# A Strassen weight gradient: loads in program order, twenty-one pairs instead of twenty, and a new plan of visits

## The chip, the cores and the metric

One core of a Trainium2 chip. The metric is the time of one execution on the device in microseconds, the median of several runs; all runs told here are in the fast state. A profiled execution gives the trace; its span is about 1.8 us shorter than the time (166.3 against 168.07 us before, 164.9 against 166.66 after), because the time also holds what lies before the first and after the last instruction. In the views PE is TensorE (matmuls; PEld its weight loads), DVE VectorE, ACT ScalarE, POOL GpSimd, which issues most loads here, and SP SyncE, which issues the outputs. The program keeps its operands and sums in tiles of one memory, SBUF, and lets PE accumulate in tiles of another, PSUM; it calls those banks. A landing is the moment at which a load's data is complete.

## The reference

```python
def setup_inputs():
    batch, m, k, n = 16, 512, 1024, 768          # fp32 normal
def reference(input, grad_output):
    return np.einsum('bmk,bmn->kn', input, grad_output).astype(np.float32)
```

So OUT (1024 x 768) = X^T G with 8192 rows. The rows are cut into 64 slices of 128. The output has four quadrants, A and B above, C and D below, each 512 x 384, which is four PSUM banks of 128 x 384 a quadrant.

## The kernel before

X and G are read as fp32 and land as bf16 (the transfer casts: of the 58.72 MB that the page counts as read from HBM, the loads issued by GpSimd take 57.28 and land as 28.64); only G of slice 0 and X of slices 0 and 1 land as fp32 and are rounded by DVE and ACT. A *plain* slice costs 16 matmuls of 384 columns, four a quadrant. A *Strassen pair* of slices costs seven products of four matmuls, 28 instead of 32, but needs six sums on DVE first. `LOADS` says which pairs of slices are plain ("s") and which are Strassen pairs ("P").

The loads and the six sums of a pair:

```python
LOADS = "ssssssssPPPPPPPPPPPPPPPPPPPPssss"
...
ctx.enter_context(tc.manual_schedule(engines={E.PE, E.DVE, E.Activation}))
...
for u, kind in enumerate(LOADS):
    ...                                   # tiles xp, gp; 14 pairs are held
    if u >= MERGED:                       # one transfer for both slices of a pair
        nc.gpsimd.dma_start(out=gp, in_=G[rows, :]...)
        nc.gpsimd.dma_start(out=xp, in_=X[rows, :]...)
    for h in range(2): ...                # otherwise one transfer a slice, first G, then X

def sum_g1(i): tensor_add(ge[:, 0:2, :], ...)    # 768 wide
def sum_g2(i): tensor_add(ge[:, 2, :], ...)      # 384
def sum_g3(i): tensor_sub(g[:, 1:3, :], ...)     # 768, in place
def sum_x1(i): tensor_add(xe[:, 0:2, :], ...)    # 1024: the "wide X sum"
def sum_x2(i): tensor_add(xe[:, 2, :], ...)      # 512
def sum_x3(i): tensor_sub(x[:, 1:3, :], ...)     # 1024, in place
```

The program has two sets of four banks only (`bank0` to `bank7`). So a quadrant or a product (m, n, o, p, q) is *visited*: it takes a set, accumulates some slices, and closes: each bank is evicted, by DVE (add into the sum in SBUF) or by ACT (copy out, after the old sum had been copied in at the opening). `ORDER` is the plan of visits. A step `3A17!3,0,0,1` reads: do 3 waiting DVE jobs first; matmuls for A up to its 17th item; close, and put 3, 0, 0 and 1 further DVE jobs ahead of the evictions of its four banks. `A21:2!...` opens A with two banks for ACT. The DVE jobs come from one list: six sums a pair, then the shares that add the products into the quadrants.

```python
def shut(q):
    fill(ahead[q])                        # DVE jobs queued ahead of this eviction
    bank, _, act = banks[q]
    dst = sum_of(p, q)
    if act:         nc.scalar.copy(out=dst, in_=bank)
    elif fresh[p]:  nc.vector.tensor_copy(out=dst, in_=bank)
    else:           nc.vector.tensor_add(out=dst, in0=bank, in1=dst)
    if final and p in "ABCD":             # last visit: the bank's part of the output leaves
        nc.sync.dma_start(out=OUT[...], in_=dst)
```

The program fixes the order of PE, DVE and ACT (`manual_schedule`), and in the trace DVE keeps to its order also where it must wait: before the change it is idle for 0.79 us ahead of an eviction at 103.24 us, though the X which the next two sums read (L149, L154) had landed before 101.77, when the wide X sum of the same pair starts. The order of the loads was left to the scheduler: at the start it puts G of slice 3 ahead of X of slice 2, then it follows the program up to pair 23, and then it takes, for example, X of pairs 24 and 25 ahead of their G.

Of the kernel before, what the change touches and what calls it, by code (L numbers as in the profile page):

```python
# [7 lines left out]

P = 128

LOADS = "ssssssssPPPPPPPPPPPPPPPPPPPPssss"



ORDER = (
    "A1:4 C1:4!0,0,0,0 B2:4!0,0,0,0 A2 D1:2 A3!0,0,0,0 D2 D3 D4 C4:4!0,0,0,0 D5 B5:2 D6!0,0,0,0 "
    "B6 A6:2 B7 B8 A7 A8 A9!0,0,0,0 B9 C9:2 C10!0,0,0,0 B11 D11:2 B12 D13!0,0,0,0 A14:2 A15 B14 "
    "B16!0,0,0,1 C16:2!2,0,1,2 A16 A17 D17:4!3,0,1,2 A18!0,0,0,0 n2:4!0,0,1,0 o1:2 m2:4 o2 "
    "2o3!3,0,0,0 m3!0,0,0,0 q3:4!1,2,0,0 p1:4 p2 p4 3D20:3!3,0,0,1 p5 q5:2!2,0,0,0 A21:2!1,0,0,2 "
    "p6 o6:2!2,0,0,1 n6:2 3p7!2,1,0,0 n7 m7:2!2,1,0,1 n8 q8:2!2,0,0,1 D24:2!2,0,1,1 n9 "  # L20
    "o9:2!2,0,0,1 A25:2 2n10!2,0,0,0 A26 m10:2!2,0,0,1 p11:2 3A27!3,0,0,0 p12 D27:2!1,0,0,2 "
    "q12:2!1,0,1,1 p13 o13:3!3,0,2,1 p14 n13:2!1,0,0,1 m14:2!1,0,1,2 p15 D30:2!2,0,0,1 "
    "A31:2!1,1,0,2 q16:2!1,1,0,1 p16 n16:2!2,1,0,0 p17 1m17:2!2,0,0,1 o17:2!2,0,0,2 D34:2!1,0,1,1 "
    "p18 p19 A34:4!4,1,1,0 p20!0,0,0,0 D35:0 o20:2!2,0,0,1 q20:2!1,0,0,1 n20:2!0,1,0,1 "
    "D37!0,0,0,0 m20:4!0,0,1,0 A35:0 A36 B19:0 B20 A39 A41 A44!11,0,0,0 B23 C17:0 B24!2,0,0,0 "
    "C24!2,0,0,0 D44:0!4,0,0,0 "
).split()


SHARES = (  # L30
    "l20 l21 t20 t21 t22 t23 t30 t31 t32 t33 t10 t11 t12 t13 l22 l23 l10 l11 l12 l13 l30 l31 l32 "
    "l33 "
).split()

WARMUP = [512] * 10 + [128] * 2
PAIRS_HELD = 14
SUMS_HELD = 9

MERGED = 8


@with_exitstack
def kernel(
# [30 lines left out]
    SLOT = {"n": 0, "p": 1, "m": 2, "o": 3, "q": 4}  # L74

    E = mybir.EngineType
    ctx.enter_context(tc.manual_schedule(engines={E.PE, E.DVE, E.Activation}))

    xf = [pairs.tile([P, K], f32, name=f"xf{s}", tag="xp") for s in range(2)]
    gf = pairs.tile([P, N], f32, name="gf", tag="gp")  # L80
# [18 lines left out]
    xg = []  # L99
    for u, kind in enumerate(LOADS):  # L100
        pool = pairs if u else head
        xp = pool.tile([P, 2, K], bf16, name="xp", tag="xp")
        gp = pool.tile([P, 2, N], bf16, name="gp", tag="gp")
        if u >= MERGED:
            rows = slice(2 * u * P, 2 * (u + 1) * P)
            nc.gpsimd.dma_start(out=gp, in_=G[rows, :].rearrange("(p m) n -> p m n", m=2))  # L106
            nc.gpsimd.dma_start(out=xp, in_=X[rows, :].rearrange("(p m) k -> p m k", m=2))  # L107
        for h in range(2):
            s = 2 * u + h
            if s > 0 and u < MERGED:  # L110
                nc.gpsimd.dma_start(out=gp[:, h, :], in_=G[s * P : (s + 1) * P, :])  # L111
            if s > 1 and u < MERGED:
                nc.gpsimd.dma_start(out=xp[:, h, :], in_=X[s * P : (s + 1) * P, :])  # L113
# [275 lines left out]
```

## Time and profile before

| | before |
|---|---|
| time, median (range) | 168.19 us (168.03 to 168.38) |
| span of the profiled run | 166.3 us |
| matmuls, with 12 for warm-up | 963 |
| PE busy, DVE busy | 159.8, 118.6 us |
| last load lands | 142.9 us |
| first matmul after warm-up starts, last starts | 5.18, 162.84 us |

The prediction below shows the lines that carry the argument. One more, part 4 of the page, the chain of waits that ended last:

```profile
PE 76%; DVE 16%; DMA 5%; POOL 1%; issue 1%; DVEq 0%; POOLq 0%
```

The chain goes through PE for three quarters and leaves it for DVE for a sixth of the span. Those are the places where a matmul waited for a sum or for an eviction.

### The profile page before, as it was taken

To read this page: it belongs to the slowest core of one execution; us is meant where nothing else is said; L and a number is where in the kernel's file an instruction comes from. 1 tells how busy PE (TensorE), PEld (TensorE's weight loads), DVE (VectorE), ACT (ScalarE), POOL (GpSimd) and SP (SyncE) were. 2 spreads that over 40 slices of the span, in tenths; PEclk is the share of its full clock that TensorE was granted. 3 is DMA by queue.
4 is the path that set the end of the run, shared out by engine and by line. 5 is a ranking of instruction groups with operands and counts; after the bars stand their busy time and mean duration, and the time that the engine had idled before them with its cause. 6 is when DMAs were issued, how large, how long until landed. Compare 5 with 4: busy or idle time off the path is not lost.

```text
span 166.3 us, 2688 instructions
## 1 busy us (share of the span) xinstructions
PE 159.8 (96%) x963; PEld 93.5 (56%) x963; DVE 118.6 (71%) x240; ACT 87.6 (53%) x206; POOL 41.1 (25%) x81
## 2 busy tenths in 40 slices
PE   8799999999999999999999999899999999999992
PEld 2356656565655655665565655455656656565661
DVE  0400221121979879878979998989999899999992
ACT  3779413330486768755648476756677878100000
POOL 7444444544122222222212222222221000000000
PEclk9999999999999999999999999999999999999999
DMA  5999999999999999999999999999999999105555
GB/s 181 287 209 208 211 206 208 208 209 217 211 216 211 215 212 214 210 215 210 215 211 214 211 213 212 217 211 212 212 217 213 214 210 209 25 0 189 189 189 189
DMA packets 14124, 33.39 MB, mean 201 GB/s; under 512 B 1568, under 2 KB 5920, under 8 KB 14112
## 3 DMA queue, kind: packets, MB, share of 16 engines
q0 software_dynamic: 11088, 28.64, 88.5%
q1 hardware_dynamic: 2736, 3.54, 6.0%
q10 hardware_dynamic: 288, 1.05, 1.7%
q8 instruction: 7, 0.11, 0.3%
q14 instruction: 5, 0.04, 0.1%
HBM read 58.72 MB, written 3.15 MB: 372 GB/s over the span
## 4 chain that ended last, share of the span: by engine, by line
PE 76%; DVE 16%; DMA 5%; POOL 1%; issue 1%; DVEq 0%; POOLq 0%
PE bank L278 75%; DVE macc L296 5%; DMA xp<-in_input_dram 5%; DVE gp L140 2%; DVE xe L145 2%; DVE acc L296 2%; DVE ge L131 2%; DVE xp L154 1%; POOL gp L111 1%; DVE ge L135 1%; DVE xe L149 1%; PE bank L328 0%; DVE acc L336 0%; DVEq L296 0%; POOLq L373 0%
## 5 line engine op out<-in xcount | busy, mean ns | idle before, releaser
L278 PEld LDWEIGHTS <-xp 128*128 128x128 bf16 x697 | 67.6, 98 | 49.4 <-issue 1.9
L278 PE MATMUL bank<-gp,xp 128*128 128x384 bf16 x537 | 92.4, 326 | 2.0 <-DVE xp L203 0.8
L292 ACT COPY acc<-bank 128x384 f32<-128x384 f32 x55 | 24.4, 487 | 31.2 <-PE bank L278 31.1
L296 DVE TENSOR_TENSOR acc<-bank,acc 128x384 f32<-128x384 f32 x46 | 23.7, 552 | 21.3 <-PE bank L278 21.0
L292 ACT COPY macc<-bank 128x384 f32<-128x384 f32 x61 | 27.3, 492 | 20.2 <-PE bank L278 20.1
L278 PEld LDWEIGHTS <-xe 128*128 128x128 bf16 x240 | 23.2, 98 | 16.6 <-DVE xe L145 1.4
L278 PE MATMUL bank<-ge,xp 128*128 128x384 bf16 x160 | 29.8, 326 | 0.2
L278 PE MATMUL bank<-gp,xe 128*128 128x384 bf16 x160 | 28.3, 326 | 0.3 <-DVE xe L145 0.2
L296 DVE TENSOR_TENSOR macc<-bank,macc 128x384 f32<-128x384 f32 x37 | 19.4, 553 | 5.3 <-PE bank L278 5.0
L107 POOL DMA_DIRECT2D xp<-in_input_dram x24 | 12.7, 530 | 36.9 <-DMA xp<-in_input_dram 20.3
L106 POOL DMA_DIRECT2D gp<-in_grad_output_dram x24 | 12.7, 530 | 32.7 <-PE bank L278 19.5
L268 ACT COPY bank<-macc 128x384 f32<-128x384 f32 x43 | 19.3, 490 | 0.0
L268 ACT COPY bank<-acc 128x384 f32<-128x384 f32 x41 | 18.4, 501 | 0.0
L163 DVE TENSOR_TENSOR acc<-acc,macc 128x768 f32<-128x768 f32 x16 | 14.5, 950 | 0.0
L145 DVE TENSOR_TENSOR xe<-xp 128x1024 bf16<-128x1024 bf16 x20 | 13.7, 684 | 0.7 <-DMA xp<-in_input_dram 0.7
L278 PE MATMUL bank<-ge,xe 128*128 128x384 bf16 x80 | 14.1, 326 | 0.0
L154 DVE TENSOR_TENSOR xp<-xp 128x1024 bf16<-128x1024 bf16 x20 | 13.7, 683 | 0.0
L131 DVE TENSOR_TENSOR ge<-gp 128x768 bf16<-128x768 bf16 x20 | 11.0, 550 | 0.1
L140 DVE TENSOR_TENSOR gp<-gp 128x768 bf16<-128x768 bf16 x20 | 11.0, 551 | 0.0
L113 POOL DMA_DIRECT2D xp<-in_input_dram x14 | 7.5, 538 | 9.0 <-DMA xp<-in_input_dram 6.4
L111 POOL DMA_DIRECT2D gp<-in_grad_output_dram x15 | 8.2, 547 | 6.1 <-DMA gp<-in_grad_output_dram 4.6
L294 DVE COPY acc<-bank 128x384 f32<-128x384 f32 x2 | 1.0, 554 | 10.6 <-PE bank L278 10.6
(19 smaller groups left out, 34.3 us busy)
## 6 DMA issues: line engine op xcount, KB each, us to landing
xp<-in_input_dram POOLq DMA_DIRECT2D x24, 512.0 KB, 16.9
gp<-in_grad_output_dram POOLq DMA_DIRECT2D x24, 384.0 KB, 16.7
xp<-in_input_dram POOLq DMA_DIRECT2D x14, 256.0 KB, 8.5
gp<-in_grad_output_dram POOLq DMA_DIRECT2D x15, 192.0 KB, 8.5
out_dram<-acc SPq DMA_DIRECT2D x15, 192.0 KB, 1.9
xf<-in_input_dram ACTq DMA_DIRECT2D x2, 512.0 KB, 5.0
gf<-in_grad_output_dram SPq DMA_DIRECT2D x2, 192.0 KB, 4.3
out_dram<-acc SPq DMA_DIRECT2D x1, 128.0 KB, 1.7
```

Of the source, the lines that this page charges most:

```text
L106: nc.gpsimd.dma_start(out=gp, in_=G[rows, :].rearrange("(p m) n -> p m n", m=2))
L107: nc.gpsimd.dma_start(out=xp, in_=X[rows, :].rearrange("(p m) k -> p m k", m=2))
L111: nc.gpsimd.dma_start(out=gp[:, h, :], in_=G[s * P : (s + 1) * P, :])
L131: nc.vector.tensor_add(out=ge[:, 0:2, :], in0=g[:, :, 0, :], in1=g[:, :, 1, :])
L140: nc.vector.tensor_sub(out=g[:, 1:3, :], in0=g[:, 1:3, :], in1=g[:, 3::-3, :])
L145: nc.vector.tensor_add(out=xe[:, 0:2, :].rearrange("p a k -> p (a k)"), in0=xp[:, 0, :], in1=xp[:, 1, :])
L154: nc.vector.tensor_sub(out=x[:, 1:3, :], in0=x[:, 1:3, :], in1=x[:, 0::3, :])
L163: nc.vector.tensor_add(out=dst, in0=dst, in1=macc[:, slots, q, :])
L268: nc.scalar.copy(out=bank, in_=sum_of(p, q))
L278: nc.tensor.matmul(bank, stat, mov, start=opening and j == 0 and not carried, stop=close and j == len(items_now) - 1, skip_group_check=car ...
L292: nc.scalar.copy(out=dst, in_=bank)
L296: nc.vector.tensor_add(out=dst, in0=bank, in1=dst)
```

## The change

Its intent: let the transfers start in the order in which the program names them (GpSimd joins the engines whose order is fixed), turn one plain pair into a twenty-first Strassen pair (four matmuls fewer), merge the transfers of slices 14 and 15 too, and plan the visits anew on the landings measured on the chip. The whole diff:

```diff
--- before.py
+++ after.py
@@ -8,35 +8,34 @@
 
 P = 128
 
-LOADS = "ssssssssPPPPPPPPPPPPPPPPPPPPssss"
+LOADS = "ssssssssPPPPPPPPPPPPPPPPPPPPPsss"
 
 
 
 ORDER = (
-    "A1:4 C1:4!0,0,0,0 B2:4!0,0,0,0 A2 D1:2 A3!0,0,0,0 D2 D3 D4 C4:4!0,0,0,0 D5 B5:2 D6!0,0,0,0 "
-    "B6 A6:2 B7 B8 A7 A8 A9!0,0,0,0 B9 C9:2 C10!0,0,0,0 B11 D11:2 B12 D13!0,0,0,0 A14:2 A15 B14 "
-    "B16!0,0,0,1 C16:2!2,0,1,2 A16 A17 D17:4!3,0,1,2 A18!0,0,0,0 n2:4!0,0,1,0 o1:2 m2:4 o2 "
-    "2o3!3,0,0,0 m3!0,0,0,0 q3:4!1,2,0,0 p1:4 p2 p4 3D20:3!3,0,0,1 p5 q5:2!2,0,0,0 A21:2!1,0,0,2 "
-    "p6 o6:2!2,0,0,1 n6:2 3p7!2,1,0,0 n7 m7:2!2,1,0,1 n8 q8:2!2,0,0,1 D24:2!2,0,1,1 n9 "
-    "o9:2!2,0,0,1 A25:2 2n10!2,0,0,0 A26 m10:2!2,0,0,1 p11:2 3A27!3,0,0,0 p12 D27:2!1,0,0,2 "
-    "q12:2!1,0,1,1 p13 o13:3!3,0,2,1 p14 n13:2!1,0,0,1 m14:2!1,0,1,2 p15 D30:2!2,0,0,1 "
-    "A31:2!1,1,0,2 q16:2!1,1,0,1 p16 n16:2!2,1,0,0 p17 1m17:2!2,0,0,1 o17:2!2,0,0,2 D34:2!1,0,1,1 "
-    "p18 p19 A34:4!4,1,1,0 p20!0,0,0,0 D35:0 o20:2!2,0,0,1 q20:2!1,0,0,1 n20:2!0,1,0,1 "
-    "D37!0,0,0,0 m20:4!0,0,1,0 A35:0 A36 B19:0 B20 A39 A41 A44!11,0,0,0 B23 C17:0 B24!2,0,0,0 "
-    "C24!2,0,0,0 D44:0!4,0,0,0 "
+    "A1:4 C1:2!0,0,0,0 D1:2 A2!0,0,0,0 D2 B3:4 D3 D4!0,0,0,0 B4 C4:2 C5 B5 C6!0,0,0,0 B6 A6:2 B7 "
+    "A8!0,0,0,0 D8:2 B8 B9 D10!0,0,0,0 B10 B11 C7:2 C9 B12 C11 B13!0,0,0,0 C12 C13 A14:2 C14 "
+    "C16!0,0,0,0 A15 B16:2!3,0,0,0 D16:2 3A17!3,0,0,1 n2:4!0,1,1,0 D17 D18 m2:4!3,0,1,0 "
+    "q3:4!1,1,1,1 D19 o1:4 o2 o3 1o4!2,1,0,0 D20!0,0,0,0 p4:4 n3:3 3p5!3,0,0,0 n4 A21:2!3,0,0,1 "
+    "n6 1m6:4!3,1,0,1 n7 o7:2!2,0,0,1 q7:2!2,0,0,2 n8 p8:2!2,0,0,1 D24:2!1,1,0,2 n9 A25:3!3,0,1,1 "
+    "n10 o10:2!2,0,0,1 m10:2 2n11!2,0,0,1 m11 q11:2!2,0,1,1 p12:2!1,1,0,2 D28:2 m12 3D29!3,0,0,0 "
+    "m13 A28:2 2m14!1,0,0,0 A30 o12:2 o13 3o15!3,0,0,1 A31 q15:2!2,1,0,2 A32!0,0,0,0 n16:2 "
+    "D32:4!6,1,1,1 p17:2 1n18!3,0,0,0 p18 m17:2 2p19!3,0,0,0 m19 D35:3!3,1,0,2 o20:2 m20 "
+    "3o21!2,0,0,0 m21!0,0,0,0 q20:2 p20:4 p21!4,1,0,0 q21!0,0,0,0 D39:0 n21:4!3,1,0,1 D41 "
+    "A37:4!2,1,1,1 D42 B17:0 D43!6,0,0,0 B19 B22!0,0,0,0 C19:0 C22!0,0,0,0 A43:0!4,0,0,0 "
 ).split()
 
 
 SHARES = (
-    "l20 l21 t20 t21 t22 t23 t30 t31 t32 t33 t10 t11 t12 t13 l22 l23 l10 l11 l12 l13 l30 l31 l32 "
-    "l33 "
+    "t10 t11 t12 t13 l20 t20 t21 t22 t23 l21 l22 l23 l10 l11 l12 l13 l30 l31 l32 l33 t30 t31 t32 "
+    "t33 "
 ).split()
 
 WARMUP = [512] * 10 + [128] * 2
 PAIRS_HELD = 14
 SUMS_HELD = 9
 
-MERGED = 8
+MERGED = 7
 
 
 @with_exitstack
@@ -74,7 +73,7 @@
     SLOT = {"n": 0, "p": 1, "m": 2, "o": 3, "q": 4}
 
     E = mybir.EngineType
-    ctx.enter_context(tc.manual_schedule(engines={E.PE, E.DVE, E.Activation}))
+    ctx.enter_context(tc.manual_schedule(engines={E.PE, E.DVE, E.Activation, E.Pool}))
 
     xf = [pairs.tile([P, K], f32, name=f"xf{s}", tag="xp") for s in range(2)]
     gf = pairs.tile([P, N], f32, name="gf", tag="gp")
```

## The prediction

> **What bounds the kernel now.** I read the page first, then the wait list and the timeline of PE, then the chain of waits, then the stretches, then when each load landed.
>
> ```profile
> PE 159.8 (96%) x963; PEld 93.5 (56%) x963; DVE 118.6 (71%) x240; ACT 87.6 (53%) x206; POOL 41.1 (25%) x81
> PEclk9999999999999999999999999999999999999999
> DMA  5999999999999999999999999999999999105555
> L278 PE MATMUL bank<-gp,xp 128*128 128x384 bf16 x537 | 92.4, 326 | 2.0 <-DVE xp L203 0.8
> ```
>
> PE is busy 96% of 166.3 us at full clock, so the whole story is matmul count plus PE gaps. The printed 326 ns is a modelled length of overlapping matmuls; the cost of one is the spacing of starts. The chain gives it in one line:
>
> ```profile
> 10.65 52.52 PE bank L278 x322
> ```
>
> 52.52 us / 322 = 163 ns; unbroken stretches of the timeline give 162.5 ns, which I use. There are 963 - 12 warm-up = 951 matmuls: 937 of 384 columns and, at the very end, 7 of 256 and 7 of 128 columns, spaced 109 and 56 ns. Work: 937 x 0.1625 + 7 x 0.165 = 153.4 us. The timeline of PE says where it starts and ends:
>
> ```profile
> 5.18 1.88 PE L278 MATMUL bank<-gp,xp 128*128 128x384 bf16 x9 [0.28 <-DVE xp L203]
> 7.61 2.83 PE L278 MATMUL bank<-gp,xp 128*128 128x384 bf16 x15 [0.56 <-DVE xp L203]
> 10.65 35.92 PE L278 MATMUL bank<-gp,xp 128*128 128x384 bf16 x220 [0.20 <-DMA xp<-in_input_dram]
> ...
> 107.82 0.81 PE L278 MATMUL bank<-gp,xp 128*128 128x384 bf16 x4 [0.55 <-DVE gp L140]
> ...
> 161.74 1.32 PE L328 MATMUL bank<-gp,xp 128*128 128x256 bf16 x14
> ```
>
> From 5.18 to 162.9 (163.06 less the 0.16 us by which a modelled end overshoots the spacing) is 157.7 us, so 4.3 us are stalls. At the start, 24 matmuls need 3.9 us and took 10.65 - 5.18 = 5.47: 1.57 us lost. The other 2.7 us lie between 62 and 125 us, as eight waits of 0.1 to 0.7 us, and DVE ends nearly all of them. The bracketed figures understate each by 0.16 us, because of the modelled ends. The wait list of PE:
>
> ```profile
> PE bank L278 <- DVE xp L203: 0.8, 2, 0.6
> PE bank L278 <- DVE gp L140: 0.7, 2, 0.6
> PE bank L278 <- DVE xe L145: 0.2, 1, 0.2
> PE bank L278 <- DMA xp<-in_input_dram: 0.2, 1, 0.2
> ```
>
> L203 rounds the first slices to bf16; L140 and L145 are Strassen sums. Two stretches show why DVE is late in the middle and that nothing is late afterwards:
>
> ```profile
> 85.00:105.00 20.00, 19.86 (x123) 11.80 (x122) 18.29 (x40) 12.46 (x30) 5.06 (x10) 1.00 1.07 212
> 125.00:145.00 20.00, 20.00 (x125) 12.04 (x123) 19.05 (x36) 13.67 (x33) 0.53 (x1) 1.00 0.89 178
> ```
>
> (us, then busy time of PE, PEld, DVE, ACT, POOL, clock, DMA share, GB/s.) DVE works 18.3 of 20 us, so a sum that stands behind an eviction in DVE's order comes late. In the tail, the last matmul is followed by two DVE adds and an output of 1.6 us: 3.4 us to the end.
>
> The loads are the second bound, almost as tight: in the middle a pair (512 KB of X, 384 KB of G as bf16, twice that read) lands every 4.31 us (X of pair 8 at 43.64, pair 9 at 47.95, pair 10 at 52.26). A Strassen pair costs PE 28 x 0.1625 = 4.55 us, a plain pair 32 x 0.1625 = 5.2 us. PE is slower, but is never more than a few us behind a landing in the middle, so it cannot be moved earlier at will.
>
> [...] sums sit idle-free in program order between L296 evictions. [...] So order changes which tile lands first, not when the last one lands; the trace has DMA at 9 in every slice up to 142.9 us, when the last load lands.
>
> **The change part by part.**
>
> *Twenty-one Strassen pairs.* One plain pair (32) becomes a Strassen pair (28): 940 instead of 944 full-size matmuls before the split of the last block. The last step spans six slices instead of seven: 934 full and 6 + 6 split. 934 x 0.1625 + 6 x 0.165 = 152.8 us: **-0.65 us**, certain, as all of it is on PE's path. It adds six DVE sums: spacing 0.47 + 0.27 + 0.47 + 0.60 + 0.33 + 0.60 = 2.74 us of DVE.
>
> *Fewer, longer visits.* The instruction order shows evictions by DVE of 39 + 29 + 4 against 46 + 37 + 4 (15 fewer at 0.47 us = -7.0 us) and by ACT of 48 + 63 against 55 + 61, reloads 79 against 84 (10 fewer copies at 0.49 = -4.9 us). With the extra sums DVE does 4.3 us less. None of that is on the path by itself; it makes late sums rarer.
>
> *The start.* Before, the third step (B2) needs slice 1, whose fp32 X lands at 7.04: that is the 0.56 gap. After, D1 takes its place and needs only slice 0, but its bank waits for C1's eviction, which now goes to DVE for two of the four banks, behind the rounding of G: 6.16 + 0.35, then two copies of 0.5 to 7.0 and 7.5. D1 starts at about 7.05 instead of 6.5, its second block at 7.55: 0.9 us of stall. Slice 1 is ready by about 8.05, as A2 comes. The program order of loads puts X of slice 2 ahead of one G transfer: it lands 0.95 us earlier, 9.65 instead of 10.60, about when B3's third matmul wants it (20 + 2 matmuls: 5.18 + 3.6 + 0.9 = 9.7). Start stall about 0.95 instead of 1.57: **-0.6 us**.
>
> *The middle.* I place each step at 5.18 + 0.1625 x (matmuls before it) + stalls so far, and compare with landing plus the DVE instructions ahead of the sum it needs. Most steps clear. Three do not:
> - n2 wants the X sum of pair 9 at 48.5 (260 matmuls, 0.95 stall). It stands behind two evictions of A17, done at 48.05 and 48.55, then 0.60: 49.15. Stall 0.6.
> - n7 (388 matmuls, at 69.85) wants the X sum of pair 14, which lands at 69.51: 0.60 later is 70.15. Stall 0.3.
> - A32 (636 matmuls, at 110.5) wants the last X sum of pair 23, landed 108.4. After it come one eviction of q15 (109.25), 0.60, another eviction (110.35), 0.33, 0.60: 111.3. Stall 0.8.
>
> With 0.25 for small ones that I do not see, 1.95 instead of 2.7: **-0.75 us**. For pairs 24 to 28, program order makes landings regular: before, X of 24 and 25 came ahead of G of 24 (115.2 us), which the new order lands at about 110.2.
>
> *Merged slices 14 and 15.* One issue of each kind fewer; a plain pair takes about 4.4 us to land in two halves, 4.3 merged. But slice 14 must wait for 15 (39.0 us); C16 wants it at 38.33 + 0.95 = 39.3. Zero.
>
> *The end.* Before, the last step gives DVE 7 x 0.1625 x 4 = 4.55 us for four subtractions (1.9) and three evictions (1.5). After it has six slices, 3.9 us, and DVE arrives late from C22's evictions by about 0.75: 4.15 us, so the last adds come later behind the last matmul: **+0.4 us**.
>
> Sum: -0.65 - 0.6 - 0.75 + 0.4 = -1.6, so 168.19 - 1.6 = **166.6 us**.
>
> **Rivals.**
> 1. *The plan works as meant and every stall goes.* Then -0.65 - 1.57 - 2.7 = -4.9, 163.3 us. For it: the plan was made on landings of a real run. Against: the three checks use landings too, and the start cannot lose D1's wait. A half way (-3 us) would be 165.2.
> 2. *The landings slip.* There are already hiccups of 0.5 to 0.9 us (X of slice 7 at 20.72 to G of slice 8 at 22.58, 1.86 against 0.95 elsewhere). Visits that follow a landing by 0.1 to 0.3 us turn each into a PE stall: +1 to +2, time 168 to 169.
> 3. *Loads in program order wait for a buffer and block those behind them.* Each load reuses the buffer of the pair fourteen earlier. For pair 24, issued near 95.6, pair 10 was last read at about 68; for pair 31, issued near 125.8, pair 17 at about 101. Over twenty us of slack: no cost expected; a failure would add several us.
> 4. *DVE becomes the end.* Its queue is full from about 145 us (subtractions, then evictions of D, B, C, A). If it lags 0.6 us more, bank reuse stops PE: +0.5 to +1.
>
> **Range and chances.** The stalls are the uncertain term: 1.7 to 4 us instead of my 2.9 (0.95 + 1.95). That gives 165.4 to 167.8. Faster by over 2% is below 164.8, which needs nearly all stalls gone and no tail cost: 6%. Slower by 2%, 171.6, needs a new stall of 4 us: 2%.
>
> **What would show it right or wrong.** PE should have 958 matmuls with warm-up. The 25th real matmul (in B3) should start near 10 us. The wait list of PE should again name DVE sums (L144, L139 or L153 after the shift of a line), with total stall of starts near 2.9 us, largest near n2 (49 us) and A32 (111 us). The last load should land within 1 us of 142.9. The last matmul should end near 161, and the end be 3.5 to 4 us later. A DMA name ahead of a long PE wait would show rival 2; POOL gaps over 3 us, rival 3; PE waits on banks after 145 us, rival 4.

## The result, and the profile after

| | before | after |
|---|---|---|
| time, median (range) | 168.19 us (168.03 to 168.38) | 166.54 us (166.38 to 166.66) |
| span of the profiled run | 166.3 us | 164.9 us |
| matmuls, with warm-up | 963 | 958 |
| DVE busy | 118.6 us | 114.3 us |
| last load lands | 142.9 us | 142.8 us |

The ratio is 0.9895, with an interval of 0.9881 to 0.991; it is the mean time of one kernel's fast runs over that of the other's of the same rounds, so not quite the ratio of the medians. By the 2% rule this is "same", by the interval a gain of 1.0%: 1.65 us against the 1.6 forecast.

The page after, first the engines, then the slices of DMA, then the chain:

```profile
PE 158.8 (96%) x958; PEld 93.8 (57%) x958; DVE 114.3 (69%) x231; ACT 83.1 (50%) x196; POOL 39.9 (24%) x79
DMA  5999999999999999999999999999999999300875
PE 91%; DVE 6%; issue 1%; DVEq 0%
```

The chain is now PE for 91% (76% before). DMA is at 9 for as long as before: no load became faster, only the order is different (X of slice 2 lands at 9.59 us instead of 10.60, the last load at 142.77 instead of 142.91). The wait list of PE has two entries in the middle (the third line below is at the start), where before there were eight waits of 0.1 us or more:

```profile
PE bank L277 <- DVE xp L153: 0.7, 1, 0.7
PE bank L277 <- DVE xe L144: 0.6, 1, 0.6
PE bank L277 <- DVE acc L293: 0.2, 1, 0.2
```

The timeline of PE shows where they are:

```profile
5.21 2.13 PE L277 MATMUL bank<-gp,xp 128*128 128x384 bf16 x8
7.50 40.27 PE L277 MATMUL bank<-gp,xp 128*128 128x384 bf16 x245 [0.16 <-DVE acc L293]
...
49.65 1.31 PE L277 MATMUL bank<-gp,xe 128*128 128x384 bf16 x7 [0.58 <-DVE xe L144]
...
111.60 0.82 PE L277 MATMUL bank<-ge,xp 128*128 128x384 bf16 x4 [0.70 <-DVE xp L153]
```

At 49.65 it is n2, which waited for the wide X sum of pair 9; at 111.60 it is A32, which waited for the in-place X sum of pair 23. The prediction named both, at 48.5 to 49.15 and 110.5 to 111.3. In spacing of starts they cost 0.74 and 0.87 us (0.6 and 0.8 forecast).

To see where the time was won, I took the start of matmul k after warm-up, counted from 0, in each trace. Up to the last block one matmul is the same work in both kernels, so a difference in these starts is a difference in stalls:

| matmul k starts at (us) | 24 | 40 | 260 | 388 | 456 | 640 | 740 | 924 | last | end of span |
|---|---|---|---|---|---|---|---|---|---|---|
| before | 10.65 | 13.26 | 49.01 | 70.39 | 82.04 | 113.01 | 129.73 | 159.63 | 162.84 | 166.30 |
| after | 10.40 | 13.00 | 48.75 | 70.30 | 81.48 | 112.26 | 128.51 | 158.41 | 160.97 | 164.87 |
| after minus before | -0.25 | -0.26 | -0.26 | -0.09 | -0.56 | -0.75 | -1.22 | -1.22 | -1.87 | -1.43 |

Three things stand out. The 0.26 us won at the start has shrunk to 0.09 at matmul 388, at 70 us: up to there the new plan waits 0.74 us at n2, the old one 0.26 and 0.32 us at its matmuls 358 and 364. The middle, from 70 to 130 us, gives 1.13 us. The fewer matmuls give -0.65 at the last one (-1.22 to -1.87). And the end gives back 0.45: from the start of the last matmul to the end of the span it was 3.46 us and is 3.90.

The last adds of DVE, before (the last row of its timeline) and after:

```profile
162.71 0.68 DVE L336 TENSOR_TENSOR acc<-bank,acc 128x256 f32<-128x256 f32 x2 [0.21 <-PE bank L328]
```

```profile
151.94 5.93 DVE L295 TENSOR_TENSOR acc<-bank,acc 128x384 f32<-128x384 f32 x12
157.78 1.95 DVE L173 TENSOR_TENSOR acc<-acc,macc 128x384 f32<-128x384 f32 x4
159.66 1.48 DVE L295 TENSOR_TENSOR acc<-bank,acc 128x384 f32<-128x384 f32 x3
161.05 0.61 DVE L335 TENSOR_TENSOR acc<-bank,acc 128x256 f32<-128x256 f32 x2
```

After, no idle time stands in brackets: DVE works through twelve evictions, four subtractions and the last evictions without a gap. Before, it sat idle 0.21 us ahead of its last two adds. As the evictions now come every 0.47 us, so do the outputs, and their issues (the last five 0.46 to 0.50 us apart in the trace) queue too: the last is issued 0.46 us after the last add, and was 0.20 before.

### The profile page after: what moved, and what is told of

It is laid out like the page before. It is cut to its first block, busy times and chain, and to the rows that moved or that the text cites. A ratio compares the mean times of both kernels' runs of the same rounds, so it can differ in the third digit from the quotient of the medians.

```text
span 164.9 us, 2645 instructions
## 1 busy us (share of the span) xinstructions
PE 158.8 (96%) x958; PEld 93.8 (57%) x958; DVE 114.3 (69%) x231; ACT 83.1 (50%) x196; POOL 39.9 (24%) x79
## 4 chain that ended last, share of the span: by engine, by line
PE 91%; DVE 6%; issue 1%; DVEq 0%
PE bank L277 88%; PE bank L88 3%; DVE acc L295 3%; DVE xe L144 1%; DVE acc L293 1%; DVE macc L295 1%; DVE acc L173 0%; DVE xp L153 0%; DVE acc L335 0%; DVE xe L148 0%; DVEq L383 0%
## 5 line engine op out<-in xcount | busy, mean ns | idle before, releaser
L277 PE MATMUL bank<-gp,xp 128*128 128x384 bf16 x514 | 88.4, 328 | 0.3 <-DVE acc L293 0.2
L295 DVE TENSOR_TENSOR acc<-bank,acc 128x384 f32<-128x384 f32 x39 | 19.9, 553 | 28.0 <-PE bank L277 27.7
L291 ACT COPY acc<-bank 128x384 f32<-128x384 f32 x48 | 21.3, 485 | 35.7 <-PE bank L277 35.2
L277 PEld LDWEIGHTS <-xe 128*128 128x128 bf16 x252 | 24.4, 98 | 17.4 <-DVE xe L144 1.5
L277 PE MATMUL bank<-ge,xp 128*128 128x384 bf16 x168 | 31.1, 327 | 0.7 <-DVE xp L153 0.7
L277 PE MATMUL bank<-gp,xe 128*128 128x384 bf16 x168 | 30.4, 327 | 0.6 <-DVE xe L144 0.6
L295 DVE TENSOR_TENSOR macc<-bank,macc 128x384 f32<-128x384 f32 x29 | 15.2, 554 | 6.6 <-PE bank L277 6.3
L267 ACT COPY bank<-acc 128x384 f32<-128x384 f32 x36 | 16.1, 497 | 0.0
L277 PE MATMUL bank<-ge,xe 128*128 128x384 bf16 x84 | 15.5, 327 | 0.0
L153 DVE TENSOR_TENSOR xp<-xp 128x1024 bf16<-128x1024 bf16 x21 | 14.4, 685 | 0.0
L148 DVE TENSOR_TENSOR xe<-xp 128x512 bf16<-128x512 bf16 x21 | 8.8, 419 | 0.0
```

The source lines that it names most:

```text
L148: nc.vector.tensor_add(out=extra[i][0][:, 2, :], in0=xp[:, 0, 0:KH], in1=xp[:, 1, KH:K])
L153: nc.vector.tensor_sub(out=x[:, 1:3, :], in0=x[:, 1:3, :], in1=x[:, 0::3, :])
L267: nc.scalar.copy(out=bank, in_=sum_of(p, q))
L277: nc.tensor.matmul(bank, stat, mov, start=opening and j == 0 and not carried, stop=close and j == len(items_now) - 1, skip_group_check=car ...
```

## The experiments

Twelve kernels ran. Ratios are against the kernel before in the same rounds; on those chips it took 168.35 to 168.41 us. The changed kernel's own ratio was 0.9895 in its rounds. "Us over the changed kernel" below are medians against its 166.54; as the kernel before took 0.16 to 0.22 us more on those chips, the ratios put each run about 0.2 us lower against the changed kernel than the medians do.

**1. The order of loads alone.** On the kernel before:

```diff
-    ctx.enter_context(tc.manual_schedule(engines={E.PE, E.DVE, E.Activation}))
+    ctx.enter_context(tc.manual_schedule(engines={E.PE, E.DVE, E.Activation, E.Pool}))
```

> The kernel before, with one word changed: loads are issued in program order, the old plan of visits stays. My theory (order is worth something only where a landing is awaited): the X of slice 2 lands about 0.95 us earlier, so the last of the start stalls (0.36 us) goes, and the waits on DVE sums between 62 and 110 us stay; time 167.8, that is -0.2 to -0.5 us. Rival (the order of loads is the whole gain of the change): 166.5 to 166.8. Second rival (the old plan leans on the early X of pairs 24 and 25): a new wait near 119 to 124 us and 168.2 to 169.

Measured: 168.38 us against 168.41, ratio 0.9999 (0.9991 to 1.0008). Nothing, so all three expectations missed: mine by 0.2 us, and the second rival's time fits but its new wait is not in the trace. X of slice 2 did land earlier, at 9.89 instead of 10.60 us, and the wait for it is gone. But the 25th matmul starts at 10.76 (10.65 before): the old plan asks for slice 1 as its third step, and there ACT's rounding of slice 1 cost 0.45 us instead of 0.21. Three of the first matmuls also stood about 0.3 us apart instead of 0.163 in this profile (see the last section), 0.43 us in all, though most of that would have been waited for anyway. The waits between 62 and 125 us are the same to 0.01 us each. So the order of loads by itself cures none of the middle, and the start had a second wait right behind the first.

**2. The new plan without the order.** The same line, taken out of the changed kernel.

> The changed kernel, but the scheduler orders the loads again. In its list two G transfers now stand ahead of the X of pair 23, and four ahead of the X of pair 26. My theory (the plan is tied to the landings): X of slice 2 lands at about 10.5 instead of 9.6 (a stall of 0.5 to 0.9 at the start), X of pair 23 at about 110.1 instead of 108.3, so the step A32 waits until about 113.3 instead of 111.6, and takes in the start stall; time 168.1 to 169, +1.6 to +2.5 us over the changed kernel. Rival (fewer evictions are what pays, order is minor): 166.4 to 166.9.

Measured: 167.85 us, ratio 0.9962 (0.9949 to 0.9976), 1.3 us over the changed kernel (1.1 by the ratios). The direction is right, the size below my range. Its wait list has a line that no other run of the new plan has in this size:

```profile
PE bank L277 <- DMA xp<-in_input_dram: 1.0, 1, 1.0
```

X of slice 2 lands at 10.92 and B's third matmul waits 1.15 us for it. X of pair 23 landed at 110.38 as I had expected, yet the wait at A32 grew only from 0.87 to 0.93 us. In the changed kernel the first X sum of pair 23 starts at 109.45, 1.2 us after the landing, as it stands behind an eviction which PE releases; here PE was 0.9 us late already, so the later landing was met almost on time. A small new wait (0.29 us, for ACT) came at 128 us. Of the 1.24 us by which the last matmul starts later than in the changed kernel's trace, 0.90 is there at the 25th matmul and still there at matmul 388: time lost at the start reaches the end. So the order is worth 1.3 us to the new plan and nothing to the old one; the two parts of the change aren't additive.

**3. Slices 14 and 15 apart again** (`MERGED = 8` in the changed kernel).

> The changed kernel with slices 14 and 15 loaded apart (merging from pair 8 as before). My theory: no wait of PE near 39 us in either form, so 166.5, within 0.2 us. Rival (merging matters for the landing rate): all later landings 0.1 us or more later, the waits on pairs 9 and 23 grow, +0.2 to +0.5 us.

Measured: 166.73 us, ratio 0.9897 (0.9878 to 0.9915): within noise of the changed kernel. Landings are 0.35 us later in its trace (X of pair 23 at 108.63 instead of 108.28) and the waits at n2, n8 and A32 are those of the changed kernel to 0.01 us. The shift is not the merging's: X of slice 2 already lands 0.43 us later. Merging is worth nothing that these rounds can tell.

**4. Four matmuls given back.** In the changed kernel, four extra matmuls in step o20, overwritten at once:

```diff
+        if n == 92:
+            for q in (0, 0, 1, 1):
+                stat, mov = operands(p, items_now[0], q)
+                nc.tensor.matmul(banks[q][0], stat, mov, start=True, stop=True)
```

> The changed kernel with four extra matmuls of 384 columns in the step o20 (at about 128 us), overwritten at once, so the result is unchanged: it gives back the four that the twenty-first Strassen pair saved. My theory (every matmul there is on the path that sets the end): +0.65 us, 167.2. Rival (slack behind the landings or DVE hides them): 0 to +0.3, 166.5 to 166.8.

Measured: 167.30 us, ratio 0.9932 (0.9916 to 0.9948). 0.9932 / 0.9895 is 0.37%, 0.62 us: four matmuls at 0.1625 are 0.65. At 128 us every matmul is on the path.

**5. The wait at n2, first try.** The wide X sum of pair 9 ahead of A17's evictions:

```diff
-3A17!3,0,0,1 n2:4!0,1,1,0
+3A17!4,0,0,0 n2:4!0,1,1,0
```

> The changed kernel with the X sum of pair 9 (the wide one) put ahead of the first eviction of A17 instead of behind the second. My theory (the 0.74 us wait at n2 is a sum queued behind two evictions, and the time goes to the end): that wait falls to under 0.15 us, the wait at A32 stays within 0.2 us of 0.87, time 165.8, -0.5 to -0.75 us. Rival (the wait only moves to A32, whose pair lands at a fixed time): n2's wait goes, A32's grows to about 1.6, time 166.5.

Measured: 166.66 us, ratio 0.9894 (0.9875 to 0.9912). No gain, and the rival is wrong too: the wait at A32 stayed at 0.86. The wait list shows what became of n2's:

```profile
PE bank L277 <- DVE acc L295: 0.5, 1, 0.5
```

n2 takes the set of banks that A17 frees. With the sum first, those evictions come later, and n2 waits for its bank instead of its operand, 0.70 us instead of 0.74. My edit had swapped one wait for the other.

**6. The wait at A32.** All X sums of pair 23 ahead of q15's evictions:

```diff
-q15:2!2,1,0,2 A32!0,0,0,0
+q15:2!5,0,0,0 A32!0,0,0,0
```

> The changed kernel with all three X sums of pair 23 ahead of the evictions of q15 instead of between and behind them. My theory (0.87 us at A32 is the queue on DVE, not the landing at 108.3 us): the wait at A32 falls to under 0.15 us, time 165.7, -0.6 to -0.9 us. Rival (the landing binds): the wait stays above 0.6 us. Second rival (the late evictions of q15 stop the bank of n16): a new wait of 0.3 us or more at n16.

Measured: 165.77 us, ratio 0.9839 (0.9818 to 0.986): -0.8 us, the wait at A32 is gone and no new one came. DVE around it, first the changed kernel, then this one:

```profile
108.98 0.56 DVE L295 TENSOR_TENSOR macc<-bank,macc 128x384 f32<-128x384 f32 x1
109.45 0.68 DVE L144 TENSOR_TENSOR xe<-xp 128x1024 bf16<-128x1024 bf16 x1
110.05 0.55 DVE L295 TENSOR_TENSOR macc<-bank,macc 128x384 f32<-128x384 f32 x1
110.52 0.42 DVE L148 TENSOR_TENSOR xe<-xp 128x512 bf16<-128x512 bf16 x1
110.85 0.69 DVE L153 TENSOR_TENSOR xp<-xp 128x1024 bf16<-128x1024 bf16 x1
```

```profile
108.71 0.69 DVE L144 TENSOR_TENSOR xe<-xp 128x1024 bf16<-128x1024 bf16 x1
109.31 0.42 DVE L148 TENSOR_TENSOR xe<-xp 128x512 bf16<-128x512 bf16 x1
109.65 0.69 DVE L153 TENSOR_TENSOR xp<-xp 128x1024 bf16<-128x1024 bf16 x1
110.25 1.01 DVE L295 TENSOR_TENSOR macc<-bank,macc 128x384 f32<-128x384 f32 x2
```

The sum that A32 needs (L153) ends at 111.54 in the first, behind two evictions of q15, and at 110.34 in the second. X of pair 23 had landed at 108.3 in both. Nobody needed the banks of q15 that early.

**7. Both moves of 5 and 6.**

> Both moves of the two single ones. Theory: the two waits are independent, the gains add up to -1.3 to -1.6 us, 165.0 to 165.3, which would be over 1.5% below the kernel before. Rival (with PE earlier by 1.6 us the landings of pairs 28 to 31 bind): a wait that names a load or the sums of pair 28 near 131 us or later, and only -0.9 us.

Measured: 165.70 us, ratio 0.9836 (0.9816 to 0.9856). Only what 6 gives. The rival I had written named pairs 28 to 31; no wait was there.

**8. The wait at n2, second try.** Another step between A17 and n2, so that both the sum and the banks have time:

```diff
-n2:4!0,1,1,0 D17 D18
+D17 n2:4!0,1,1,0 D18
```

> The changed kernel with the step D17 (which needs only pair 8) put ahead of n2 instead of behind it, so that the X sum of pair 9 has 0.65 us more and the banks that A17 frees are not asked for at once. Theory A (the wait at n2 is lost time): it falls under 0.1 us and the time by 0.5 to 0.7, to 165.9. Theory B, after the first try at n2 gained nothing (PE at 50 to 75 us runs at the pace of the landings, whatever is saved at n2 is waited for again at pairs 10, 11 or 14): n2's wait goes, waits of 0.1 to 0.4 us show at q3, D20 or n7, and the time stays within 0.2 us of 166.5.

Measured: 166.65 us, ratio 0.9903 (0.9887 to 0.9918): theory B. The wait at n2 fell from 0.74 to 0.09 us. In its place came 0.26 at q3, 0.36 at D20 and 0.29 at n7. Two lines of PE (D20, n7) and one of DVE ahead of n7:

```profile
58.20 0.82 PE L277 MATMUL bank<-ge,xp 128*128 128x384 bf16 x4 [0.20 <-DVE xp L153]
...
70.19 0.82 PE L277 MATMUL bank<-gp,xe 128*128 128x384 bf16 x4
```

```profile
69.44 0.69 DVE L144 TENSOR_TENSOR xe<-xp 128x1024 bf16<-128x1024 bf16 x1 [1.14 <-DMA xp<-in_input_dram]
```

DVE had been idle 1.14 us when X of pair 14 landed (69.42 us), and n7 can start only after that sum. Matmul 388 is n7's first in the new plan. In six profiles it waits, for 0.12 to 0.38 us (experiments 3, 5, 7, 8, 11 and 12), and there it starts 0.74 to 0.76 us after the wide X sum of pair 14 does. In experiments 4, 6, 9 and 10 it starts at most 0.1 us later than that. The changed kernel's own profile has more room (one line of DVE, one of PE):

```profile
69.18 0.69 DVE L144 TENSOR_TENSOR xe<-xp 128x1024 bf16<-128x1024 bf16 x1 [0.58 <-DMA xp<-in_input_dram]
```

```profile
70.30 0.81 PE L277 MATMUL bank<-gp,xe 128*128 128x384 bf16 x4
```

Here n7 starts 1.12 us after the sum, so that by the 0.75 us of the others about 0.37 us could be saved ahead of it; in experiments 8 and 11 what was saved beyond that was waited for at n7. A delay is not absorbed: in experiment 2 n7 starts at 71.20.

**9. DVE's work given back.** In the changed kernel, seven extra adds of 384 columns on DVE between 65 and 105 us:

```diff
         def shut(q):
+            if q == 0 and n in (54, 57, 60, 64, 68, 72, 79):
+                nc.vector.tensor_add(out=scratch, in0=scratch, in1=scratch)
             fill(ahead[q])
```

> The changed kernel with seven extra adds of 384 columns on DVE (0.47 to 0.55 us each) between 65 and 105 us, which gives back the 3 us of DVE work that the stretch from 62 to 125 us lost against the kernel before. Theory (the lighter DVE is what keeps the sums on time there): new waits on DVE sums between 65 and 110 us, 0.7 to 2 us together, time 167.2 to 168.3. Rival (DVE's slack of 13% holds them, the plan's places for the sums are what matters): under 0.3 us, 166.5 to 166.8.

Measured: 167.18 us, ratio 0.9928 (0.9916 to 0.994), 0.6 us over the changed kernel: between the two expectations. The stretch of the middle (us, then busy PE, PEld, DVE, ACT, POOL, clock, DMA, GB/s) before, after, and here:

```profile
62.00:125.00 63.00, 61.68 (x373) 35.89 (x371) 57.98 (x123) 41.28 (x96) 15.36 (x29) 1.00 1.07 213
```

```profile
62.00:125.00 63.00, 62.30 (x384) 37.11 (x382) 54.90 (x117) 37.98 (x89) 15.30 (x29) 1.00 1.07 213
```

```profile
62.00:125.00 63.00, 61.93 (x381) 36.69 (x379) 57.21 (x123) 37.98 (x89) 15.31 (x29) 1.00 1.07 213
```

With nearly the old DVE load (57.2 of 58.0 us), one wait grew, at n8, from 0.12 to 0.51 us; the wide X sum of pair 15 starts at 75.31 instead of 74.88, one extra add later. The other six adds cost nothing. So the lighter DVE is worth at most about 0.4 us of the 1.1 in the middle, in these seven places; for the rest, better places of the sums in the queue are the candidate left, which no run here shows by itself.

**10. The tail.** The eight subtractions of 384 columns that stand late in DVE's queue, on GpSimd:

```diff
-        nc.vector.tensor_sub(out=c, in0=c, in1=macc[:, 4, q, :])     # L173, and L184 likewise
+        nc.gpsimd.tensor_sub(out=c, in0=c, in1=macc[:, 4, q, :])
```

> The changed kernel with the eight last 384-wide subtractions (L173, L184) on GpSimd instead of DVE. My theory of the tail (DVE runs without a gap from 134.6 us to the last add, 161.7, and squeezes the last outputs to the spacing of their issues): with 8 x 0.47 us less on DVE, DVE comes free before the last step, the last add ends within 0.5 us of the last matmul (0.64 now), the last output is issued sooner, time -0.2 to -0.45 us, 166.1 to 166.3. Rival (PE sets the end): 166.5. Second rival (GpSimd takes over 1.5 us for one and the evictions wait for it): slower by 0.5 us or more.

Measured: 166.45 us, ratio 0.9881 (0.9862 to 0.99): -0.1 us by the medians and -0.2 by the ratios, inside the noise of its rounds and at best at the edge of what I expected. The trace shows that DVE does come free:

```profile
153.88 4.27 DVE L295 TENSOR_TENSOR acc<-bank,acc 128x384 f32<-128x384 f32 x9 [0.40 <-POOL acc L184]
...
160.27 0.56 DVE L295 TENSOR_TENSOR acc<-bank,acc 128x384 f32<-128x384 f32 x1 [0.42 <-PE bank L277]
160.92 0.62 DVE L335 TENSOR_TENSOR acc<-bank,acc 128x256 f32<-128x256 f32 x2
```

DVE now waits for PE in the last step, and the last output is issued 0.26 us after the last add (0.46 after the change). But the last add ends 0.61 us after the start of the last matmul (0.70), so this run takes only 0.1 off the lateness of DVE's last add. From the start of the last matmul to the end of the span it is 3.75 us, and 3.90 in the changed kernel; but 1.27 of the 3.75 come after the last landing, and 1.09 to 1.10 in the changed kernel and in experiments 11 and 12, for a reason that stays open. GpSimd's first subtraction took 3.38 us and the other seven 1.00 each: the first began at 147.59 us, while DVE ran its shares, and ended at 150.97, 0.86 us after the last of them (150.11). No run here shows why it took longer.

**11. A candidate**: moves of 6 and 8, and B's first visit split so that eight matmuls on slices 0 and 1 come ahead of slice 2 (`B3:4` becomes `B2:4 B3`).

> A candidate for a better version: X sums of pair 23 ahead of q15's evictions, D17 ahead of n2, and B's first visit split so that eight matmuls on slices 0 and 1 run before slice 2 is asked for. Under theory B of the n2 run, the first is worth -0.85 us and the others nothing: 165.7. Under theory A: 165.0 or less.

Measured: 165.64 us, ratio 0.9838 (0.9825 to 0.9851), theory B to the tenth. The split does what it should at the start (the 25th matmul at 9.77 us instead of 10.40), and matmul 388 is at 70.04: of the 0.63 us, 0.26 is left, with 0.38 us of waiting at n7.

**12. The candidate with the last four subtractions on GpSimd.**

> The same candidate with the last four subtractions (L173) on GpSimd: as the other tail run gave about -0.1 us, 165.5 to 165.6, at most 0.3 us below the candidate without it.

Measured: 165.35 us, ratio 0.9823 (0.981 to 0.9837); its output is correct. That is 0.15 us below the expected 165.5, and 0.3 below experiment 11 as the bound allowed, though the two intervals overlap. It is the fastest of all: 1.2 us below the changed kernel, 3.0 below the one before on that chip. From the last matmul's start to the end of the span it takes 3.58 us, 3.90 in experiment 11, and the last output is issued 0.25 us after the last add, 0.46 there.

## Why the prediction was right, point by point

The time (166.6 forecast, 166.54 measured), the range and the class held. (The upper end of the range should have been 167.7: 4 us of stalls are 1.1 more than 2.9.) By its own steps:

- **Four matmuls fewer, -0.65 us.** Right: -0.65 from matmul 924 to the last, and 0.62 us when four were given back.
- **The start, -0.6.** The landing of X of slice 2 (9.65 forecast, 9.59 measured) and D1's wait for DVE's evictions are there, two gaps of 0.32 and 0.30 us. The size was off: 0.26 us in the profile, where the first four matmuls stood 0.32 us apart instead of 0.163. In the profiles of experiments 3 to 10, which have the same start, the 25th matmul starts at 9.98 to 10.40 us, 0.25 to 0.67 earlier than before. And not all of it can reach the end. I had noted that PE "cannot be moved earlier at will" and did not apply it to my own first term: experiments 8 and 11 show n7 waiting for pair 14, whose X lands at 69.2 to 69.6 us in the profiles of the new plan with loads in program order. The 0.09 at matmul 388 is no sign of that: in this trace n7 waits for nothing, and the difference went at n2.
- **The middle, -0.75.** The waits at n2 and A32 came where and as large as forecast. The wait at n7 (0.3) did not: X of pair 14 landed at 69.16 instead of 69.51, and PE came 0.4 us later; 0.12 at n8 did. In total the stalls after the start were 1.72 us against 1.95 forecast and 2.7 before.
- **Together** the start and the middle were to give -1.35, and gave -1.22 up to matmul 924. The division was off, the sum nearly right: the start gave 0.34 less than forecast and the middle 0.22 more, which is luck.
- **The queue on DVE, not the landing, makes A32 wait.** Right: moving the sum takes 0.8 us off (experiment 6), and a landing 2.1 us later changed the wait by 0.06 (experiment 2), which weighs less, as PE came 0.9 us later there too.
- **The tail, +0.4.** Right in size, +0.45, and half named in its reason. The last add is 0.15 later behind the last matmul, and the issues of the outputs, which queue behind each other, are 0.26; I had not named those. Both shrink when DVE has less to do: the tail of experiment 12 is 0.32 us shorter than that of experiment 11.
- **Merging, zero; buffers, no wait.** Right: experiment 3, and no load waited longer than before.
- **The rivals.** All stalls gone: no, though experiment 12 shows that a good half of what it asked for was to be had. Landings that slip: no wait of PE in the changed kernel's trace comes from one, and the last is at 142.8. Program order stopping the loads: no. DVE as the end: it is the end of the chain from 155.8 us, but at a cost of tenths, and no wait for a bank appeared after 145 us.

What stays open: how the 1.13 us of the middle divide between the lighter DVE and the better places of the sums. Experiment 9 loads seven places of many. The old plan could not be given the new places without becoming the new plan.

## What to carry to other kernels

Here PE was within 3% of its work, and the gain of the new plan was the number of matmuls plus the stalls; a stall is best read as "which instruction stands ahead of the needed one in an in-order queue": moving three sums past two evictions was worth 0.8 us, half of the whole change. Before crediting a saving, look for the next point downstream that a landing pins, here n7 behind pair 14 at 69 us: a step that starts at one distance from a landing in trace after trace, whatever came before it. A table of the k-th matmul's start in both traces shows where a difference collapses, but only the waits in between tell why: here it was n2, not the landing. A fix at a wait can hand the time to the bank, the operand or the landing behind it (0.70 us at the bank of n2 in experiment 5, 0.29 at n7 behind a landing in experiment 8), so ask of each wait what would end it next.

## What else the traces show of the hardware

- An unbroken stream of weight loads and matmuls of 384 columns took 162.5 ns a matmul in every trace here (in experiment 6, 16 from 63.62 to 66.22 us). At the end of the trace before, matmuls of 256 columns stand 109 ns apart and those of 128 columns 56 ns.
- 12 warm-up matmuls fill 4.4 us, and the next one to four were still spaced about 270 to 320 ns instead of 163 in six of the fourteen profiles. In the changed kernel's, the spacing of 320 ns ended at 6.5 us, 5.7 us after the first matmul; its four matmuls cost 0.63 us at that place, while the clock line of the profile showed 9. In the trace before, the first matmuls after warm-up, from 5.18 us, were at 163 to 173 ns at once.
- The stream of 512 and 384 KB loads (as bf16, cast from twice that), in which each load starts about 0.3 to 0.9 us after the one eight before it has landed, read 1.84 MB every 4.31 us, 426 GB/s, and landed in order of issue in the traces before and after.
- At the end of the changed kernel, the last five outputs, issued one after another from one queue, were issued 0.46 to 0.50 us apart, and the last one stood 0.26 us longer behind the last add than before.
